# A two-layer attention block on one core: score and max matmuls on 64-row halves of the TensorE array

## The chip, the cores and the metric

One core of a Trainium2 chip runs the whole program. The metric is device time in microseconds. The kernel before took 3601.7 us (median of 3 runs, 3600.24 to 3606.74).

## What is computed

Two layers over 2048 latent tokens and 256 context tokens of width 1024. In each layer one projection feeds four branches of 256 columns: MLA attention (4 heads), GQA attention (4 heads, 2 key heads), a chunked gMLP and a Fourier mix. Each is multiplied by a gate, and one output projection follows. The change touches attention alone:

```python
def attend(q, k, v):
    ...
        s = jnp.einsum("bqkgd,blkd->bkgql", qblk, k).astype(jnp.float32) * scale
        pr = jax.nn.softmax(s, axis=-1).astype(v.dtype)
        return jnp.einsum("bkgql,blkd->bqkgd", pr, v)
```

Latent queries read latent and context keys (2304) in one softmax; in the first layer context queries read the context keys as well. An MLA head has 64 plain and 32 rotary columns in query and key, a GQA head has 64; values have 64 columns in both. The scores must be close to fp32, since the gains are large.

## The kernel before, in words

**Stages.** A layer projects its tokens (gMLP, MLA, GQA, gates, Fourier input), writes queries, keys, values and gates to DRAM (`QKA`, `QB`, `KB`, `V1`, `V2`, `G`), runs `attention()` (L1071), and then projects the output (`out_block`, L1268). Queries and keys are kept as a high and a low part, both in a format that TensorE takes in one pass ("fp32r"), so that a score is q_hi k_hi + q_lo k_hi + q_hi k_lo.

**Blocks.** Attention goes through 16 blocks per layer (L1005): four pairs of heads (pairs 0 and 1 MLA, 2 and 3 GQA) by four blocks of 512 queries. A block loops over 18 key tiles of 128 keys (L1212). For each key tile and each of the two heads e of the pair, `scores` (L1115) makes a 128x512 score in a PSUM bank of tag "s" (three banks), and ACT takes its exponential into a tile `p`. An MLA head needs three matmuls of 96 or 100 rows. A GQA head puts q_hi and q_lo on 128 rows over k_hi twice, so it needs two matmuls, of 128 and 68 rows. Four of the rows (two for a context block) hold minus the row maximum on the query's side and ones on the key's side, so the maximum is subtracted in the matmul.

**Maximum.** The maximum for block n+1 is worked out during block n: `max_units` (L952) makes one unit for each head, each of four query tiles and each of five key chunks (four of 512, one of 256): one matmul into a bank "m" (three banks) and one `reduce_max` on VectorE (L976), with a small reduce after five of them (L980). `row` (L989) transposes the maxima with TensorE and writes them negated into the query tile.

**Values and sums.** After every third key tile `drain` (L1154) runs the value matmuls of these three tiles (L1110): the two heads write partitions 0 to 63 and 64 to 127 of one bank "o" (two banks). The exponentials are added up over the key tiles in `acc` (`sums`, L1139): 34 adds per block, 6 (MLA) or 8 (GQA) on VectorE, the others on GpSimd. `fin` (L1159) sums `acc` over partitions with a matmul of ones, ACT copies that, VectorE takes the reciprocal in two halves (L1170) and multiplies by the values (L1174), GpSimd multiplies by the gate (L1175), and the result goes to DRAM.

**Order.** On TensorE, VectorE and GpSimd the order of instructions in the attention is the program's order (L1246). Max units and, in the first three blocks, units of the Fourier branch (`fnet`, L725) are spread between the score steps as `fill` (L1218). The previous block's `fin` stands after key tile 5 and its tail is spread over the steps behind. In the first layer the last block of each pair also carries a small block of the context queries (`ctx_units`). All DMAs are issued on SP's queue. `prep` (L1007) loads a pair's keys (`load_k`, L902) and a block's queries (`load_q`, L938); the first block's are loaded during the projection stage before, where its max units run as well (L1062 to L1068).

Of the kernel before, what the change touches and what calls it, by code (L numbers as in the profile page):

```python
# [28 lines left out]
PBUF = 10  # L29

# [6 lines left out]
def kernel(  # L37
# [13 lines left out]
    ps = ctx.enter_context(tc.tile_pool(name="ps", bufs=1, space=PSUM))  # L51
# [23 lines left out]
    NB = {"s": 3, "m": 3, "o": 2}  # L75

    def bank(tag, shape):
        return ps.tile(shape, F32, tag=tag, name=f"ps_{tag}", bufs=NB[tag])

# [3 lines left out]
    def f32(ap):  # L83
        return ap.bitcast(F32)
# [293 lines left out]
    def layer(l, xin, shs, hxs, xss, c):  # L378
# [511 lines left out]
        def load_kc():  # L890
            kv.a = big([100, 8, 256], F32R)
            load(f32(kv.a)[0:96], KA[:, :, SEQ:T])
            load(f32(kv.a)[96:100].rearrange("o a b -> o (a b)"), onesd)

        def load_kbc():
            kv.b = wk("kb2", [P, 2, 2, 256], F32R, bufs=1)
            load(f32(kv.b)[0:64, 0], KB[0:64, :, 0, SEQ:T])
            load(f32(kv.b)[64:128, 0], KB[0:64, :, 0, SEQ:T])
            load(f32(kv.b)[0:64, 1], KB[:, :, 1, SEQ:T])
            load(f32(kv.b)[64:68, 1].rearrange("o a b -> o (a b)"), onesd[:, 0:512])  # L900

        def load_k(pair):  # L902
            r = W()
            r.pair = pair
            if pair < 2:
                kh, kl = [], []
                for e in range(2):
                    h = 2 * pair + e
                    t = big([100, SEQ], F32R)
                    load(f32(t)[0:96], KA[:, 2 * h, 0:SEQ])  # L910
                    load(f32(t)[96:100], onesd)
                    kh.append(t)
                    t = big([96, SEQ], F32R)
                    load(f32(t), KA[0:96, 2 * h + 1, 0:SEQ])
                    kl.append(t)

                def kk(e, sel, rows, s0, n):
                    if s0 < SEQ:
                        return (kl if sel == "l" else kh)[e][0:rows, s0:s0 + n]
                    h = 2 * pair + e  # L920
                    return kv.a[0:rows, 2 * h + (sel == "l"), s0 - SEQ:s0 - SEQ + n]
            else:
                g = pair - 2
                t1 = big([P, SEQ], F32R)
                load(f32(t1)[0:64], KB[0:64, g, 0, 0:SEQ])
                load(f32(t1)[64:128], KB[0:64, g, 0, 0:SEQ])
                t2 = big([68, SEQ], F32R)
                load(f32(t2)[0:64], KB[:, g, 1, 0:SEQ])
                load(f32(t2)[64:68], onesd)

                def kk(e, sel, rows, s0, n):
                    if s0 < SEQ:
                        return (t2 if sel == "l" else t1)[0:rows, s0:s0 + n]
                    return kv.b[0:rows, int(sel == "l"), g, s0 - SEQ:s0 - SEQ + n]
            r.kk = kk
            return r

        def load_q(pair, q0, nq):  # L938
            qt = big([P, 4, 512], F32R)
            if pair < 2:  # L940
                load(f32(qt)[0:96, :, :nq], QA[:, 4 * pair:4 * pair + 4, q0:q0 + nq])
            else:
                g = pair - 2
                hs = slice(2 * g, 2 * g + 2)
                load(f32(qt)[0:64, 0::2, :nq], QB[:, hs, 0, q0:q0 + nq])
                load(f32(qt)[64:128, 0::2, :nq], QB[:, hs, 1, q0:q0 + nq])
                load(f32(qt)[0:64, 1::2, :nq], QB[:, hs, 0, q0:q0 + nq])
            return qt
# [3 lines left out]
        def max_units(blk, qt):  # L952
            kp, q0, nq, keys = blk
            pair = kp.pair
            units = []
            if len(keys) == 18:
                chunks = [(i * 512, 512) for i in range(4)] + [(SEQ, 256)]
            else:
                chunks = [(SEQ, 256)]
            nch = len(chunks)  # L960
            for e in range(2):
                mt = sm(4)

                def one(e, qi, mt):
                    mx = sm(5)
                    ops = []
                    for ci, (s0, n) in enumerate(chunks):
                        def f(ci=ci, s0=s0, n=n):
                            pm = bank("m", [P, 512])
                            rows = 96 if pair < 2 else P  # L970
                            nc.tensor.matmul(  # L971
                                pm[:, :n], qt[0:rows, 2 * e, qi * P:(qi + 1) * P],
                                kp.kk(e, "h", rows, s0, n), start=True, stop=True,
                            )
                            dst = mx[:, ci:ci + 1] if nch > 1 else mt[:, qi:qi + 1]
                            nc.vector.reduce_max(out=dst, in_=pm[:, :n], axis=AX.X)  # L976
                        ops.append(f)
                    if nch > 1:
                        def g():
                            nc.vector.reduce_max(out=mt[:, qi:qi + 1], in_=mx[:, 0:nch], axis=AX.X)  # L980
# [472 lines left out]
```

## Time and profile before

| | |
|---|---|
| median of 3 runs | 3601.7 us |
| the profiled execution | 3603.65 us |
| its span in the trace | 3601.9 us |
| TensorE busy | 94% |
| VectorE, GpSimd, ScalarE busy | 58%, 50%, 35% |
| mean granted TensorE clock | 0.974 of full |

The span runs from the first to the last instruction that the profiler shows. A TensorE instruction's end is modelled: in a dense stream the next one begins before it, and the distance from start to start is what one costs. PEld is the loading of weights on TensorE. SPq, POOLq and the like are an engine's sequencer, which issues DMAs. "L1127" is a line of the kernel before; "A" is any tile of the large arena, "s" a small one.

### The profile page before, as it was taken

The numbers are of one execution on the slowest core, as the hardware profiler recorded it, in microseconds if no ns is written. First come the engines' busy times: TensorE is split into PE (matmuls) and PEld (weight loads), VectorE is DVE, ScalarE is ACT, GpSimd is POOL, SyncE is SP. The second block draws the span as 40 slices with busy tenths as digits, with TensorE's granted clock in tenths as the row PEclk, the third lists the DMA queues.
The fourth block names the chain that finished last, engine by engine and source line by source line (L and its number), as shares of the span: only waits on it lengthen the run. The fifth ranks groups of instructions, "written<-read, shape, count | busy, mean of one in ns | idle before, by whom it ended". The sixth has DMA issues, their size and how long they took to land. (4 is left out here: it accounts for less than half of the span.)

```text
span 3601.9 us, 44855 instructions
## 1 busy us (share of the span) xinstructions
PE 3370.7 (94%) x15660; PEld 2373.4 (66%) x15660; DVE 2090.4 (58%) x3694; ACT 1278.0 (35%) x2616; POOL 1818.1 (50%) x1660
## 2 busy tenths in 40 slices
PE   6999999999999999899999998999999999999999
PEld 4888788665656555455778877876555655555487
DVE  4374337359866677784343744362887666778631
ACT  4253324113234344443123534330333444444410
POOL 2433233216566678775334334242455677877722
PEclk9999999999999999999999999999999999999999
DMA  6154314751251120003351443156314212001132
GB/s 214 37 139 128 110 45 130 240 171 59 84 123 30 29 72 24 26 12 118 139 167 46 131 129 112 50 140 177 133 50 115 62 28 73 18 21 35 40 129 92
DMA packets 252609, 331.34 MB, mean 92 GB/s; under 512 B 21408, under 2 KB 168352, under 8 KB 247720
## 3 DMA queue, kind: packets, MB, share of 16 engines
q1 hardware_dynamic: 252384, 328.49, 30.7%
q8 instruction: 123, 2.02, 0.2%
q14 instruction: 102, 0.84, 0.1%
HBM read 222.22 MB, written 106.20 MB: 91 GB/s over the span
## 5 line engine op out<-in xcount | busy, mean ns | idle before, releaser
L1151 POOL TENSOR_TENSOR acc<-acc,p 128x512 f32<-128x512 f32 x800 | 1058.9, 1343 | 407.7 <-ACT p L1132 235.0
L1132 ACT ACTIVATE p<-ps_s 128x512 f32<-128x512 f32 (+1 forms) x1168 | 681.0, 595 | 968.7 <-PE ps_s L1127 927.8
L976 DVE TENSOR_REDUCE s<-ps_m 128x1 f32<-128x512 f32 (+1 forms) x1296 | 767.0, 626 | 265.3 <-PE ps_m L971 256.4
L1127 PE MATMUL ps_s<-A 96*128 96x512 f32 (+2 forms) x2776 | 835.7, 408 | 1.6 <-ACT p L1132 0.9
L1127 PEld LDWEIGHTS ps_s<-A 96*128 96x128 f32 (+2 forms) x2776 | 498.5, 191 | 255.3 <-issue 157.5
L1110 PE MATMUL ps_o<-p,A 128*64 128x512 f32 x2048 | 494.9, 615 | 0.0
L971 PE MATMUL ps_m<-A 128*128 128x512 f32 (+2 forms) x1160 | 433.3, 401 | 61.1 <-DVE s L976 54.4
L358 PE MATMUL ps_s<-A 128*128 128x512 f32 (+1 forms) x864 | 336.9, 390 | 14.3 <-DVE sg L392 6.3
L360 PE MATMUL ps_s<-A 128*128 128x512 f32 (+1 forms) x864 | 334.0, 387 | 7.0 <-POOL A L343 7.0
L359 PE MATMUL ps_s<-A 128*128 128x512 f32 (+1 forms) x864 | 333.4, 386 | 0.0
L971 PEld LDWEIGHTS ps_m<-A 96*128 96x128 f32 (+1 forms) x1160 | 221.6, 191 | 167.3 <-DVE s L976 113.5
L1151 DVE TENSOR_TENSOR acc<-acc,p 128x512 f32<-128x512 f32 x224 | 249.1, 1112 | 120.4 <-POOL acc L1151 90.9
L1110 PEld LDWEIGHTS ps_o<-p,A 128*64 128x64 f32 x2048 | 142.0, 140 | 258.2 <-issue 256.0
L352 PE MATMUL ps_s<-A 128*128 128x256 f32 (+2 forms) x848 | 292.0, 345 | 3.5 <-ACT vst L629 1.3
L353 PE MATMUL ps_s<-A 128*128 128x256 f32 (+2 forms) x848 | 286.8, 338 | 1.9 <-POOL A L327 1.6
L354 PE MATMUL ps_s<-A 128*128 128x256 f32 (+2 forms) x848 | 284.4, 336 | 2.9 <-POOL A L308 2.9
L1304 POOL TENSOR_TENSOR A<-A,d 128x512 f32<-128x512 f32 x68 | 88.7, 1306 | 266.0 <-DVE d L1303 250.2
L308 POOL TENSOR_TENSOR A<-t,A 128x512 fp32r<-128x512 f32 (+1 forms) x80 | 100.6, 1264 | 231.1 <-DVE A L307 223.4
L1296 PE MATMUL ps_s<-A 128*128 128x512 f32 x544 | 212.5, 391 | 1.3 <-ACT A L1277 1.2
L1298 PE MATMUL ps_s<-A 128*128 128x512 f32 x544 | 211.7, 390 | 0.0
L1297 PE MATMUL ps_s<-A 128*128 128x512 f32 x544 | 211.5, 389 | 0.0
L358 PEld LDWEIGHTS ps_s<-A 128*128 128x128 f32 x864 | 167.6, 194 | 54.2 <-DVE sg L392 9.3
(188 smaller groups left out, 4562.5 us busy)
## 6 DMA issues: line engine op xcount, KB each, us to landing
st<-in_w_in SPq DMA_DIRECT2D x144, 256.0 KB, 3.0
QKA<-A SPq DMA_DIRECT2D x34, 768.0 KB, 5.5
A<-QKA SPq DMA_DIRECT2D x34, 768.0 KB, 7.0
A<-in_w_mod SPq DMA_DIRECT2D x24, 1024.0 KB, 7.9
A<-X SPq DMA_DIRECT2D x17, 1024.0 KB, 6.9
A<-in_x SPq DMA_DIRECT2D x16, 1024.0 KB, 5.1
st<-Y SPq DMA_DIRECT2D x64, 256.0 KB, 3.5
G<-sg SPq DMA_DIRECT2D x48, 256.0 KB, 2.3
```

The lines of the kernel that those rows point to most:

```text
L352: nc.tensor.matmul(pt[:, :n], hx(0, k)[:, js], hi(k), start=(k == 0), stop=False)
L353: nc.tensor.matmul(pt[:, :n], hx(0, k)[:, js], lo(k), start=False, stop=False)
L354: nc.tensor.matmul(pt[:, :n], hx(1, k)[:, js], hi(k), start=False, stop=(k == KD - 1))
L358: nc.tensor.matmul(pt[:, :n], wt[:, 0, k, :], hx(0, k), start=(k == 0), stop=False)
L359: nc.tensor.matmul(pt[:, :n], wt[:, 0, k, :], hx(1, k), start=False, stop=False)
L360: nc.tensor.matmul(pt[:, :n], wt[:, 1, k, :], hx(0, k), start=False, stop=(k == KD - 1))
L971: nc.tensor.matmul(pm[:, :n], qt[0:rows, 2 * e, qi * P:(qi + 1) * P], kp.kk(e, "h", rows, s0, n), start=True, stop=True,)
L976: nc.vector.reduce_max(out=dst, in_=pm[:, :n], axis=AX.X)
L1110: nc.tensor.matmul(z.po[64 * e:64 * e + 64, :nq], vtile(pair, e, keys[i]), pts[e][:, :nq], start=(i == 0), stop=(i == nk - 1),)
L1127: nc.tensor.matmul(s[:, :nq], kp.kk(e, sel, rows, k0, P), qt[0:rows, qi, :nq], start=(m == 0), stop=(m == len(seq) - 1),)
L1132: nc.scalar.activation(p[:, :nq], s[:, :nq], AF.Exp, bias=0.0, scale=1.0)
L1151: eng.tensor_tensor(z.acc[e][:, :nq], old[:, :nq], p[:, :nq], op=ALU.add)
```

## The change

Each pair's two heads now lie on the two halves of the partitions: head e on partitions 64e to 64e+63, for queries and keys, high and low part. Every score and max matmul has at most 64 rows, and the matmuls of the two heads are issued in turn, into one bank each.

- **Scores** (`scores(i)`, both heads at once): an MLA score has five matmuls per head: plain columns hi x hi, q_lo x k_hi, q_hi x k_lo; the rotary columns as 32 high and 32 low rows in one; and the rotary q_hi x k_lo together with the rows of the maximum (36 rows). A GQA score has four: the three products of 64 rows, and one of 36 rows with only the maximum (its keys are the constant tile `kv.z`).
- **Max units** come in pairs of heads, 18 units per block: 16 of one query tile and 512 keys for both heads (MLA four matmuls, GQA two, two banks, two reduces), and 2 of two query tiles and 256 keys. GQA maxima are of the high parts alone. The row of the maximum is made at the end of the block for both heads.
- **Banks** during the attention: four "s" (were three), three "m", one "o" (were two). ACT copies the values from PSUM into a tile `po` after a block's last drain. The PSUM pool is closed and opened anew around the attention.
- **Sums**: in the first three blocks all 34 adds are on GpSimd; later 5 (MLA) or 8 (GQA) are on VectorE, those of key tiles 2, 5, 8, 11 and 14.
- **Loads**: an MLA pair's keys take 12 DMAs (6 before), the context keys 24 (2 before), an MLA query block 8 (1 before), a GQA query block 4 (3 before). The gate is loaded in `fin`.

```diff
+        def load_mla_k(dst, pair, s0, n):
+            for e in range(2):
+                h, b0 = 2 * pair + e, 64 * e
+                d = [f32(t)[b0:b0 + 64] for t in dst]
+                s = slice(s0, s0 + n)
+                load(d[0], KA[0:64, 2 * h, s])
+                load(d[1], KA[0:64, 2 * h + 1, s])
+                load(d[2][0:32], KA[64:96, 2 * h, s])
+                load(d[2][32:64], KA[64:96, 2 * h, s])
+                load(d[3][0:32], KA[64:96, 2 * h + 1, s])
+                load(d[3][32:36], onesd[:, 0:n])
...
+            def mm(pm, c0, qi, s0, n):
+                seq = (0, 2) if pair < 2 else (0,)
+                for sel in seq:
+                    for e in range(2):
+                        nc.tensor.matmul(
+                            pm[e][:, c0:c0 + n], qt[64 * e:64 * e + 64, sel, qi * P:(qi + 1) * P],
+                            kp.kk(e, sel, 64, s0, n), start=(sel == 0), stop=(sel == seq[-1]),
+                        )
+            def chunk(qi, ci, mx):
+                pm = new()
+                mm(pm, 0, qi, ci * 512, 512)
+                for e in range(2):
+                    nc.vector.reduce_max(out=mx[:, qi % 2, e, ci:ci + 1], in_=pm[e], axis=AX.X)
...
-                        seq = (("h", 96 + nqt, 2 * e), ("h", 96, 2 * e + 1), ("l", 96, 2 * e))
+                        seq = ((0, 0, 64), (0, 1, 64), (1, 0, 64), (2, 2, 64), (3, 3, 32 + nqt))
                     else:
-                        seq = (("h", P, 2 * e), ("l", 64 + nqt, 2 * e + 1))
-                    for m, (sel, rows, qi) in enumerate(seq):
-                        nc.tensor.matmul(
-                            s[:, :nq], kp.kk(e, sel, rows, k0, P), qt[0:rows, qi, :nq],
-                            start=(m == 0), stop=(m == len(seq) - 1),
-                        )
+                        seq = ((0, 0, 64), (0, 1, 64), (1, 0, 64), (2, 2, 32 + nqt))
+                    for m, (sel, qi, rows) in enumerate(seq):
+                        for e in range(2):
+                            nc.tensor.matmul(
+                                ss[e][:, :nq], kp.kk(e, sel, rows, k0, P),
+                                qt[64 * e:64 * e + rows, qi, :nq],
+                                start=(m == 0), stop=(m == len(seq) - 1),
+                            )
...
+                    if z.pend[-1][0] == nk - 1:
+                        z.ps = wk("po", [P, 512])
+                        nc.scalar.copy(z.ps[:, :nq], z.po[:, :nq])
...
+                dve = {(i, 1) for i in (2, 5, 8, 11, 14)}
                 if n < 3:
...
+                    dve = set()
+                elif pair >= 2:
+                    dve |= {(i, 0) for i in (2, 8, 14)}
...
                 for i in range(18):
...
+                    z.scores(i)
+                    want = min(len(fill), -(-len(fill) * (i + 1) // 17))
+                    while done < want:
+                        fill[done]()
+                        done += 1
+                    z.sums(i - 1)
...
+        banks_close()
+        banks_open(f"pa{l}", s=4, m=3, o=1)
         with scope(f"a{l}"), tc.manual_schedule(engines=ordered):
             attention()
+        banks_close()
+        banks_open(f"pp{l + 1}", **PROJ)
```

## Rows read from the trace of the kernel before

**Rows 1.** The page: busy time of each engine, share of the span, instructions.

```profile
PE 3370.7 (94%) x15660; PEld 2373.4 (66%) x15660; DVE 2090.4 (58%) x3694; ACT 1278.0 (35%) x2616; POOL 1818.1 (50%) x1660
```

**Rows 2.** Windows: us, busy PE PEld DVE ACT POOL, clock, DMA (Fourier, MLA, GQA block).

```profile
877.51:944.95 67.44, 60.58 (x259) 35.67 (x259) 58.51 (x87) 22.11 (x37) 40.83 (x30) 0.97 0.16 51
...
2880.65:2933.78 53.13, 52.58 (x226) 32.12 (x227) 35.00 (x60) 22.10 (x38) 36.47 (x30) 1.00 0.12 30
3091.04:3138.43 47.39, 45.24 (x191) 25.06 (x191) 38.11 (x62) 22.66 (x39) 38.14 (x30) 1.00 0.07 23
```

**Rows 3.** Chain of waits, 2800 to 2940 us (MLA): start, us, what.

```profile
by line: PE ps_s L1127 43.4%; PE ps_o L1110 30.8%; PE ps_m L971 13.7%; DVE s L976 3.7%; DVE rd L1170 2.4%; PE ps_m L1162 2.3%; DVE acc L1151 1.9%; issue 1.7%; PE ps_m L993 0.4%
...
2809.62 2.73 PE ps_o L1110 x12
2812.34 0.90 PE ps_s L1127 x3
```

**Rows 4.** Chain of waits, 3060 to 3190 us (GQA).

```profile
by line: PE ps_o L1110 29.0%; PE ps_s L1127 23.9%; DVE s L976 14.2%; PE ps_m L971 12.5%; DVE acc L1151 6.4%; issue 4.0%; POOL acc L1151 3.2%; DVE rd L1170 2.5%; PE ps_m L1162 2.5%; DVE A L995 0.5%; DVE s L980 0.5%; ACT p L1132 0.5%; PE ps_m
...
3091.04 1.08 PE ps_m L1162 x4
```

**Rows 5.** Timeline in an MLA block: start, us, engine, line, operation, tiles.

```profile
2850.95 0.39 PE L971 MATMUL ps_m<-A 96*128 96x512 f32 x1
...
2851.18 0.86 PE L1127 MATMUL ps_s<-A 100*128 100x512 f32 x3
...
2851.88 0.39 PE L971 MATMUL ps_m<-A 96*128 96x512 f32 x1
...
2852.31 0.69 DVE L976 TENSOR_REDUCE s<-ps_m 128x1 f32<-128x512 f32 x1 [0.21 <-PE ps_m L971]
...
2852.81 0.28 PE L971 MATMUL ps_m<-A 96*128 96x256 f32 x1
...
2852.93 0.39 PE L1127 MATMUL ps_s<-A 100*128 100x512 f32 x1
```

**Rows 6.** Timeline: a drain's first weight loads, and the score behind it.

```profile
2846.26 0.20 PEld L1110 LDWEIGHTS ps_o<-p,A 128*64 128x64 f32 x4 [0.25 <-issue]
...
2848.98 0.97 PE L1127 MATMUL ps_s<-A 100*128 100x512 f32 x3
```

**Rows 7.** Weight loads by shape, whole span: busy us, mean ns.

```profile
L1127 PEld LDWEIGHTS ps_s<-A 96*128 96x128 f32 x1168 | 223.8, 192 | 41.7
...
L1127 PEld LDWEIGHTS ps_s<-A 68*128 68x128 f32 x512 | 98.0, 191 | 14.1
```

**Rows 8.** Timeline in a projection stage: 256-column matmuls.

```profile
137.38 0.28 PE L353 MATMUL ps_s<-A 128*128 128x256 f32 x1
137.50 0.28 PE L354 MATMUL ps_s<-A 128*128 128x256 f32 x1
```

**Rows 9.** Groups in the GQA block 3091.04 to 3138.43: busy us, mean ns | idle before.

```profile
L976 DVE TENSOR_REDUCE s<-ps_m 128x1 f32<-128x512 f32 (+1 forms) x41 | 23.7, 621 | 4.6 <-PE ps_m L971 4.5
...
L1166 ACT COPY rd<-ps_m 128x512 f32<-128x512 f32 x1 | 0.6, 586 | 1.3 <-PE ps_m L1162 1.3
```

**Rows 10.** Groups in the Fourier block 877.51 to 944.95.

```profile
L1151 DVE TENSOR_TENSOR acc<-acc,p 128x512 f32<-128x512 f32 x6 | 5.2, 869 | 2.6 <-POOL acc L1151 2.6
...
L1151 POOL TENSOR_TENSOR acc<-acc,p 128x512 f32<-128x512 f32 x27 | 38.3, 1435 | 27.3 <-ACT p L1132 16.6 <-DVE acc L1151 10.6
```

**Rows 11.** Waits in the same Fourier block: us, times, longest.

```profile
PEld ps_m L971 <- DVE s L976: 8.4, 11, 2.0
```

**Rows 12.** Timeline of SP's queue before the attention and at a pair switch.

```profile
711.83 0.34 SPq L892 DMA_DIRECT2D A<-QKA  x1
...
740.89 1.07 SPq L341 DMA_DIRECT2D st<-in_w_in  x2
...
988.31 0.39 SPq L910 DMA_DIRECT2D A<-QKA  x1
```

**Rows 13.** Timeline of TensorE at the switch to the second pair.

```profile
1002.11 0.50 PE L971 MATMUL ps_m<-A 96*128 96x512 f32 x1 [2.04 <-DMA A<-QKA]
```

More of the change, by code (lines that the diff above doesn't have):

```diff
@@ new lines, in max_units, with row @@
+            units = []
+            for q2 in range(0, nqt, 2):
+                mx = None
+                if len(keys) == 18:
+                    mx = sm(20).rearrange("p (a e c) -> p a e c", a=2, e=2)
+                    units += [
+                        lambda qi=qi, ci=ci, mx=mx: chunk(qi, ci, mx)
+                        for qi in (q2, q2 + 1) for ci in range(4)
+                    ]
+                units.append(lambda q2=q2, mx=mx: tail(q2, mx))
+            def row():
+                px = bank("m", [P, 512])
+                for e in range(2):
+                    nc.tensor.transpose(px[0:nqt, e * P:(e + 1) * P], mt[:, 4 * e:4 * e + nqt], ident)
+                for e in range(2):
+                    r = 64 * e + 32
+                    dst = qt[r:r + nqt, 3 if pair < 2 else 2, :nq].rearrange("r (a t) -> r a t", a=nqt)
@@ L999, in row @@
                     )
[L1000 to L1003 removed]
+            return units, row
         blocks = [(pair, qb) for pair in range(4) for qb in range(4)]
@@ L1113, in av, with scores @@
                         )
[L1115 to L1120 removed]
+                def scores(i):
+                    ss = [bank("s", [P, 512]) for _ in range(2)]
                     k0 = keys[i] * P
                     if pair < 2:
[L1123 removed]
+                        seq = ((0, 0, 64), (0, 1, 64), (1, 0, 64), (2, 2, 64), (3, 3, 32 + nqt))
@@ L1141, in sums @@
+                    pts = []
+                    for e in range(2):
+                        p = wk("p", [P, 512], bufs=PBUF)
+                        nc.scalar.activation(p[:, :nq], ss[e][:, :nq], AF.Exp, bias=0.0, scale=1.0)
+                        pts.append(p)
+                    z.pend.append((i, pts))
+                    z.sum.append((i, pts))
+                def sums(upto):
+                    while z.sum and z.sum[0][0] <= upto:
+                        i, pts = z.sum.pop(0)
                         for e, p in enumerate(pts):
@@ L1184, in ctx_units @@
                 z = main_units(blk, qt)
-                return mu + [row] + [
-                    lambda i=i, e=e: z.scores(i, e) for i in range(2) for e in range(2)
-                ] + [z.sums, z.drain], z
+                return mu + [row] + [lambda i=i: z.scores(i) for i in range(2)] + [
+                    lambda: (z.sums(1), z.drain("m"))
+                ], z
             nxt = first_max
```

216 lines of the change are left out of this document (83 added, 133 removed).

## The prediction
> **What bounds the kernel now.** I read the page first: TensorE is busy 3370.7 of 3601.9 us, no other engine over 58% [rows 1]. "Busy" is modelled here, so I then read the attention stage, the only one the change touches, block by block. Sixteen blocks per layer: eight of the MLA heads (the first three also carry the Fourier work; I call these Fourier blocks), then eight of the GQA heads. One Fourier block lasts 67.44 us, a plain MLA block 53.13, a GQA block 47.39, at a granted clock of 0.97, 1.00 and 1.00 (2.4 GHz) [rows 2]. The chain of waits over plain MLA blocks is 90% TensorE [rows 3]; over GQA blocks VectorE has some 23% of it (14.2 + 6.4 + 2.5) [rows 4].
>
> What TensorE's time consists of is read from start to start, not from durations. Four matmuls of 512 columns (three of a score, one of a max) take 2850.95 to 2851.88 = 0.93 us, so a **slot is 0.2325 us**; a 256-column one takes 2852.81 to 2852.93 = 0.12 [rows 5]. A drain of values, twelve matmuls, takes 2.72 us up to the next score [rows 3], that is 0.45 per pair: the two heads' 64-column halves run side by side already, and its first four weight loads fit into 0.20 us [rows 6]. Now the sum. An MLA block: scores 18 x 6 = 108 slots, max 32 slots and 8 halves (36), together 144 x 0.2325 = 33.5 us; six drains 16.3; sums and transposes 1.3 (the sums' 1.08 in [rows 4]). That is 51.1 of 53.13, so 2.0 us of waiting. A GQA block: 72 + 36 = 108 slots = 25.1 us, with 17.6 the same makes 42.7 of 47.39: 4.7 us of waiting. A Fourier block has 51.1 and about 3.5 of Fourier matmuls, so 12.8 us of waiting.
>
> **The change part by part.** *Scores.* An MLA score goes from three matmuls per head (six slots) to five 64-row matmuls per head, ten in five pairs. If a pair costs one slot, 18 x (6 - 5) = 18 slots per MLA block are saved. A GQA score goes from four slots to four pairs: nothing. *Max.* An MLA unit takes two pairs where two slots stood: nothing. A GQA unit takes one pair where two slots stood: (32 + 8/2) - (16 + 4/2) = 18 slots per GQA block. So 16 x 18 + 16 x 18 = 576 slots x 0.2325 = **-134 us** over both layers.
>
> All of this hangs on what a pair costs. No row shows two 64-row matmuls. Bounds: below, one slot, 0.2325 (nearest row: the column halves, which run side by side in [rows 6]); above, both in turn, 0.465. I take 0.2325, since the column halves are nearest in kind, and there even the loads overlap. What could spoil it is the loads: every pair needs two. A weight load of 96 or 68 rows takes 192 and 191 ns [rows 7], so fewer rows do not make it shorter, and 256-column matmuls, each with a load, start every 0.12 us [rows 8], so a load occupies at most 0.12. Two in turn are at most 0.24, about the slot. "TensorE: Matmul & The Clock Gate" of the Trainium skill (LDWEIGHTS) says the same against this change: the time goes by columns, not rows, P/1.2 ns. By it I estimate 107 ns a load and 213 a pair: inside the slot of a 512-column pair, but not of a 256-column one; by that page the sum would be 8 x 0.09 us worse per MLA block, half that per GQA block, some 17 us in all.
>
> The break-even is simple. Per layer the new program has 8 x (90 + 36 + 72 + 18) = 1728 pairs, the old 2016 slots; the change gains while a pair costs less than 0.2325 x 2016/1728 = **0.271 us**.
>
> *Mode changes.* Going from values to scores costs little now: twelve matmuls at 2.73 and the next score 2.72 after their start [rows 3]. Scores and max units are both 64-row, so there are no more changes per drain than before; bounds 0 and 0.1 us at each Fourier unit, under 2 us in all, nothing.
>
> *VectorE and GpSimd.* A block's max reduces go from 32 full, 8 half and 8 tiny to 36 full and 2 tiny: 23.7 us [rows 9] becomes 22.4 (at the mean 0.621) to 24.8 (at 0.69 [rows 5]), and six tiny ones fall away: between -2.3 and +1.1, I take -1. GQA adds stay eight on VectorE, MLA goes from six to five: nothing. So in a GQA block VectorE would have some 37 us and GpSimd 38 beside a TensorE of 38.5 [rows 2, 9]. That is tight. A unit now needs two of three max banks, and two reduces (1.24 us) are longer than a GQA step of five slots (1.16); the 0.24 us lost in three steps is caught up in the drain of 2.72. I therefore keep the 4.7 us of waiting as it is; bounds 2 and 9.
>
> In Fourier blocks all 34 adds go to GpSimd. VectorE loses six at 869 ns (5.2 us) and 2.6 us of waiting for GpSimd; GpSimd gets six at 1435 ns, 8.6 on 40.8, still far below the block [rows 2, 10]. TensorE waits there for VectorE's reduces (8.4 us of its loads' waits in [rows 11]), so a lighter VectorE shortens the block beyond the slots. Between 0 and 5.2 us for each of six blocks; I take 2.3: **-14 us**.
>
> *One values bank, ACT copy.* Each block gains one ACT copy of 0.59 us [rows 9]; ACT is busy 22.66 of 47.39 [rows 2], and the bank is needed three score steps later: hidden. If ACT were late, the first drain would wait; nothing suggests it. The last multiply now reads SBUF beside GpSimd, as the adds do that take 0.869 us [rows 10]: once per block, off the path.
>
> *DMAs.* A layer's first block issues 24 + 12 + 8 loads where 2 + 6 + 1 stood; SP takes 0.34 to 0.54 us for each [rows 12], so 35 x 0.45 = 16 us more on SP, ahead of the Fourier weights on the same queue. Between 711.83 and 741.96 SP issues only these nine loads and a few stores and weights, so most of it fits: between 0 and 16 us per layer, I take 4. At the switch to the second MLA pair a buffer comes free late (988.31) and TensorE already waits 2.04 us for a load at 1002.11 [rows 12, 13]. Now both heads' rows must be there and fourteen issues follow where four stood: 10 x 0.45, less what overlaps: 0 to 10, I take 4. Two layers: **+16 us**. GQA loads: four and four, where four and three stood: nothing. Opening and closing the banks: a wait of at most a drain at each of four places, in the range.
>
> **Sum:** -134 - 14 + 16 = -132 on the profiled execution's 3603.65 us (span 3601.9 and 1.75 around it) = 3471.6. It lies 2 us above the median of 3601.7, so the forecast for the median is **3470 us**. Blocks: plain MLA 53.1 to 48.9, GQA 47.4 to 43.2, Fourier 67.4 to 61.
>
> **Rivals.** *VectorE and GpSimd become the bound in the GQA blocks.* For: 37 and 38 us against 38.5, and VectorE in 23% of the chain now. Against: they have idle time there at present, because TensorE holds them up. If VectorE keeps its idle 9.3 us (47.4 - 38.1), a GQA block is 37 + 9.3 = 46.3 and saves 1.1, not 4.2: 16 x 3.1 = 50 us back, **3520 us**. Chance 0.15.
>
> *The pair costs more than 0.271 us* (slower). Place: every score and max. Mechanism: the second load is not hidden behind the matmul beside it. What an unhidden load costs is seen after a drain: the first score's three matmuls take 0.97 us there against 0.86 elsewhere, 0.11 more [rows 5, 6]. One such bite per pair gives 0.34: 2 x (1728 x 0.34 - 2016 x 0.2325) = +238, about **3840 us**. Against it: loads of column halves overlap. The same page of the Trainium skill (Part 3, Packing small matmuls) reports four row tiles at 3.07 times, not 4; by it I estimate 0.2325 x 4/3.07 = 0.303 a pair, +110 us; no row here shows it. Chance of this rival 0.14, the case below taken in.
>
> *The change doesn't do what it says:* the halves take turns, 0.465 a pair: 2 x (1728 x 0.465 - 468.7) = +670, **4270 us**. Speaks against: the column halves. Chance 0.03 of the 0.14.
>
> **Numbers.** A measurement of this kernel can tell about 0.2%, 7 us, from no change. Forecast 0.68; VectorE/GpSimd rival 0.15; pair over 0.271 0.14; a pair within a few ns of break-even, no change, 0.03. Faster 0.83, same 0.03, slower 0.14. Range: downwards GQA waiting at 2 (-43), Fourier blocks at their bound (-17) and DMAs free (-16) would make 3394 together, I take 3400; upwards the first rival's 3520 with page and DMA bounds on top, 3545. That leaves the slower cases out.
>
> **What would show it.** In the changed profile: a score's two heads' matmuls start within some 0.01 us of each other, and pairs follow every 0.23 us; ten score matmuls of an MLA step in 1.16 us. Plain MLA blocks at 49, GQA at 43, Fourier at 61; the first max after the pair switch some us later than now. Wrong if pairs stand over 0.27 apart, if VectorE's share of the chain over GQA blocks rises past a half, or if SP's queue delays the Fourier weights by more than a few us.

## The result, and the profile after

The changed kernel takes 3641.0 us at the median (3635.2 to 3643.7), the kernel before 3601.0 in the same runs: a ratio of 1.0106 with an interval of [1.0089, 1.0124], **slower by 1.1%** where 3.7% faster was forecast. The profiled execution has a span of 3638.0 us against 3601.9. First the page's busy times and the windows of three blocks of the same kinds as in [rows 1, 2] (us, busy PE PEld DVE ACT POOL, clock, DMA):

```profile
PE 3323.8 (91%) x18644; PEld 2325.6 (64%) x18644; DVE 2095.3 (58%) x3320; ACT 1246.7 (34%) x2652; POOL 1861.5 (51%) x1712
```

```profile
898.00:967.00 69.00, 56.97 (x373) 34.26 (x371) 57.70 (x70) 20.73 (x38) 49.34 (x36) 0.95 0.14 45
2864.80:2915.00 50.20, 48.89 (x342) 29.32 (x340) 37.08 (x49) 20.74 (x38) 37.37 (x31) 1.00 0.19 47
3115.40:3162.10 46.70, 41.91 (x264) 23.03 (x262) 36.16 (x52) 21.75 (x40) 36.85 (x30) 1.00 0.08 26
```

TensorE is busy 47 us less and the span is 36 us longer. The plain MLA block lost 2.9 us, the GQA block 0.7; the Fourier blocks rose in sum. The timeline of TensorE in an MLA block (start, us, line, tiles, count; compare [rows 5]) shows the pairs themselves:

```profile
2893.31 1.31 PE L1141 MATMUL ps_s<-A 64*128 64x512 f32 x10
2894.45 0.63 PE L973 MATMUL ps_m<-A 64*128 64x512 f32 x4
2894.92 1.31 PE L1141 MATMUL ps_s<-A 64*128 64x512 f32 x10
```

Ten score matmuls take 2893.31 to 2894.45, 1.14 us for five pairs or 0.228 a pair, four max matmuls 0.47. In the trace the two matmuls of a pair start 3 or 4 ns apart, and so do their weight loads. So the pairs do here what was forecast, and the loss is elsewhere. From the first value matmul of a block to that of the next, summed over both layers:

| part | forecast, us | measured, us |
|---|---|---|
| plain MLA, 10 intervals | -42 | -34.6 |
| GQA, 14 intervals | -59 | -4.4 |
| Fourier, 6 intervals | -38 | +20.8 |
| up to the first score, 2 layers | +4 in each layer (0 to +16) | +30.2 and +25.3 |

These make +37.3; the other stretches are 1.2 us shorter. In the second layer the last row counts from the last value matmul of the first layer.

**GQA.** The waits of the GQA block (us, times, longest), then of the same block kind before:

```profile
PEld ps_m L973 <- DVE s L985: 6.1, 7, 2.3
DVE acc L1165 <- POOL acc L1165: 5.2, 3, 1.8
...
PE ps_m L973 <- DVE s L985: 4.0, 4, 2.0
```

```profile
PEld ps_m L971 <- DVE s L976: 3.4, 5, 1.4
DVE acc L1151 <- POOL acc L1151: 3.0, 2, 1.6
...
PE ps_m L971 <- DVE s L976: 1.5, 2, 1.0
```

TensorE's max matmuls wait more for VectorE's reduces, and VectorE more for GpSimd's running sum. In the chain over GQA blocks, TensorE, which led it with 68% in [rows 4], has 11% left:

```profile
by line: issue 37.8%; POOL acc L1165 18.4%; DVE s L985 10.7%; DVE acc L1165 8.2%; PE ps_s L1141 5.2%; PE ps_o L1127 3.7%; DVE rd L1190 3.4%; DVE s L992 2.5%; DVE A L1302 2.5%; PE ps_m L973 2.2%; DMA st<-Y 1.7%; POOL A L1284 1.0%; DVE A L101
```

VectorE's share is about a quarter, as before; GpSimd's rose from 3 to 18%. For "issue" the profile shows no wait, so this chain says less than the one before.

**Fourier.** VectorE no longer adds there, and yet is busy 57.7 us where it was 58.5 [rows 2]. Groups of the Fourier block after (busy us, mean ns):

```profile
L746 DVE TENSOR_TENSOR A<-A 128x512 f32<-128x512 f32 x12 | 13.9, 1177 | 0.0
L805 DVE SCALAR_TENSOR_TENSOR A<-A 128x512 f32<-128x512 f32 x6 | 8.0, 1349 | 0.1
...
L839 DVE SCALAR_TENSOR_TENSOR A<-st,A 128x512 f32<-128x512 f32 x2 | 3.5, 1738 | 0.0
```

In the same block of the kernel before (865.1 to 934.6 us) these operations, as many of each, took 1146, 1134 and 1087 ns. TensorE waits 11.1 us there for reduces. From start to start its scores take 23.9 us (30.5 before) and its max matmuls 23.3 (16.1 before): what the pairs save, the waits in front of the max matmuls take back.

**The entry**, from the first max matmul to the first score, lies mostly in the projection stage before attention. Windows of it, kernel before and kernel after:

```profile
740.00:760.00 20.00, 17.57 (x78) 13.39 (x71) 7.94 (x20) 1.17 (x2) 5.08 (x4) 0.91 0.50 141
760.00:780.00 20.00, 20.00 (x90) 16.16 (x89) 12.76 (x27) 3.31 (x6) 0.00 (x0) 1.00 0.82 280
```

```profile
740.00:760.00 20.00, 12.51 (x53) 8.04 (x45) 3.65 (x10) 0.92 (x2) 2.51 (x2) 0.82 0.89 196
760.00:780.00 20.00, 20.00 (x53) 11.78 (x52) 7.25 (x13) 1.17 (x2) 2.55 (x2) 0.67 0.35 128
```

TensorE idles for keys (3.55 us, timeline below, and 1.5 us more behind it); from 756.3 to 773.3 us the granted clock is at the lower of its two levels, 1.2 of 2.4 GHz, and in the second window 53 matmuls run where 90 ran. Then the max units stand among 128-row matmuls, and both heads' rows must be complete before the first score (kernel after, SyncE's queue in the second line; then kernel before):

```profile
756.22 0.77 PE L973 MATMUL ps_m<-A 64*128 64x512 f32 x1 [3.55 <-DMA A<-QKA]
756.19 1.23 SPq L346 DMA_DIRECT2D st<-in_w_in  x2
...
778.22 0.40 PE L713 MATMUL ps_o<-A,f 128*128 128x512 f32 x1
778.54 0.73 PE L973 MATMUL ps_m<-A 64*128 64x512 f32 x2
779.20 0.50 PE L714 MATMUL ps_o<-A,f 128*128 128x512 f32 x1
779.63 0.73 PE L973 MATMUL ps_m<-A 64*128 64x512 f32 x2
...
816.28 0.38 PE L1013 MATMUL ps_m<-ident,s 128*4 128x128 f32 x2 [1.59 <-DVE s L997]
818.29 1.22 PE L1141 MATMUL ps_s<-A 64*128 64x512 f32 x4 [1.63 <-DVE A L1017]
```

```profile
787.36 0.86 PE L971 MATMUL ps_m<-A 96*128 96x512 f32 x3
788.05 0.63 PE L1127 MATMUL ps_s<-A 100*128 100x512 f32 x2
788.54 0.39 PE L971 MATMUL ps_m<-A 96*128 96x256 f32 x1
...
790.26 0.27 PE L993 MATMUL ps_m<-ident,s 128*4 128x128 f32 x1 [1.10 <-DVE s L980]
```

At 778.54 two max matmuls of one head run without partner: with one 128-row matmul they take 778.54 to 779.63, 1.09 us, and not three slots of 0.2325. The Fourier weights are issued at 756.19 us, where [rows 12] had 740.89. From first max to first score it is 62.1 us (first layer) and 58.3, where it was 36.6 and 36.7. Before, 39 of the 40 max matmuls of both heads stood ahead of the first score and took 8.75 us; only the second head's row came behind it (790.26). An MLA unit now has two max matmuls per head, so both heads have 80; only 16 and 20 of the 40 pairs start together, and the 80 take 24.1 and 21.7 us.

### The profile page after: what moved, and what is told of

It reads as the page before. It is cut to its first block, busy times and chain, and to the rows that moved or that the text cites. A ratio compares the mean times of both kernels' runs of the same rounds, so it can differ in the third digit from the quotient of the medians.

```text
span 3638.0 us, 50869 instructions
## 1 busy us (share of the span) xinstructions
PE 3323.8 (91%) x18644; PEld 2325.6 (64%) x18644; DVE 2095.3 (58%) x3320; ACT 1246.7 (34%) x2652; POOL 1861.5 (51%) x1712
## 5 line engine op out<-in xcount | busy, mean ns | idle before, releaser
L1165 POOL TENSOR_TENSOR acc<-acc,p 128x512 f32<-128x512 f32 x846 | 1101.9, 1336 | 326.1 <-ACT p L1149 302.6
L1149 ACT ACTIVATE p<-ps_s 128x512 f32<-128x512 f32 (+1 forms) x1168 | 629.4, 593 | 924.6 <-PE ps_s L1141 870.6
L985 DVE TENSOR_REDUCE s<-ps_m 128x1 f32<-128x512 f32 x1024 | 643.1, 679 | 265.9 <-PE ps_m L973 263.4
L1141 PE MATMUL ps_s<-A 64*128 64x512 f32 (+1 forms) x4456 | 679.8, 410 | 3.2 <-DVE A L1017 3.2
L1141 PEld LDWEIGHTS ps_s<-A 64*128 64x128 f32 x4456 | 441.6, 190 | 231.1 <-issue 161.0
L1127 PE MATMUL ps_o<-p,A 128*64 128x512 f32 x2048 | 503.8, 623 | 4.3 <-ACT p L1149 4.3
L973 PE MATMUL ps_m<-A 64*128 64x512 f32 (+1 forms) x1808 | 383.6, 407 | 104.9 <-DVE s L985 91.4
L363 PE MATMUL ps_s<-A 128*128 128x512 f32 (+1 forms) x864 | 340.3, 394 | 16.3 <-DVE A L347 6.5
L973 PEld LDWEIGHTS ps_m<-A 64*128 64x128 f32 x1808 | 223.1, 195 | 199.9 <-DVE s L985 143.8
L1165 DVE TENSOR_TENSOR acc<-acc,p 128x512 f32<-128x512 f32 x178 | 238.0, 1358 | 144.1 <-POOL acc L1165 144.0
L348 POOL TENSOR_TENSOR A<-st,A 128x512 fp32r<-128x512 f32 x64 | 84.8, 1336 | 220.5 <-DVE A L347 179.3
```

The costliest lines, as they stand in the source:

```text
L363: nc.tensor.matmul(pt[:, :n], wt[:, 0, k, :], hx(0, k), start=(k == 0), stop=False)
L973: nc.tensor.matmul(pm[e][:, c0:c0 + n], qt[64 * e:64 * e + 64, sel, qi * P:(qi + 1) * P], kp.kk(e, sel, 64, s0, n), start=(sel == 0), stop ...
L985: nc.vector.reduce_max(out=mx[:, qi % 2, e, ci:ci + 1], in_=pm[e], axis=AX.X)
L1127: nc.tensor.matmul(z.po[64 * e:64 * e + 64, :nq], vtile(pair, e, keys[i]), pts[e][:, :nq], start=(i == 0), stop=(i == nk - 1),)
L1141: nc.tensor.matmul(ss[e][:, :nq], kp.kk(e, sel, rows, k0, P), qt[64 * e:64 * e + rows, qi, :nq], start=(m == 0), stop=(m == len(seq) - 1),)
L1149: nc.scalar.activation(p[:, :nq], ss[e][:, :nq], AF.Exp, bias=0.0, scale=1.0)
```

## The experiments

Each is an edit of the changed kernel. Ratios are against the kernel before, in the same runs.

**Order of the entry's loads** (e1), **TensorE's order in the entry** (e2), **five adds back to VectorE** (e3).

```
 if hi_ == 1:
-    load_kc()
+    wts = [load_coltile(l, 2144 + P * i) for i in range(2)]
     first_max = prep_block(0)
+    load_kc()
```

> The changed kernel, with only the order of three loads before the attention changed: first the weights of the Fourier projection, then keys and queries of block 0, then the context keys. Theory (the many loads on SP's queue make the first max and these weights late, TensorE idles and its clock falls): the first score comes 10 to 16 us earlier in each layer, the kernel falls by 20 to 32 us to about 3610 to 3620. Rival (the entry is long because max matmuls are mixed with 128-row matmuls): under 4 us per layer, the kernel stays above 3630.

Ratio 1.0136 [1.0087, 1.0185]. The first score comes 5 us earlier in the first layer (813.4) and, counted from the first layer's last value matmul, 7.3 in the second: between theory and rival. The whole has nothing of it. In the first layer the first value matmul comes 7.5 us later than in the changed kernel (834.0 for 826.6), since TensorE now waits behind the first score, 3.8 us for keys and 6.4 for reduces. The last query load is issued at 754.5 us (755.1 in the changed kernel): one queue is as late whichever loads stand first.

```
+with tc.manual_schedule(engines={mybir.EngineType.PE}):
     stage_f(hxs, full, fill)
```

> The changed kernel, with TensorE's order in the Fourier projection of the second half fixed to the program's order, so that both heads' max matmuls stand next to each other and three units follow in a row. Theory (unpaired heads and a change of tiling at nearly every max matmul): from first max to first score 62 us becomes 44 to 50 in the first layer and 58 becomes 44 to 50 in the second, the kernel falls by 20 to 28 us. Rival (VectorE's reduces set the pace there): TensorE waits for banks instead, under 6 us per layer.

Ratio 1.0144 [1.0115, 1.0174]. Entry 58.9 and 57.6 us; the changes of tiling fell from 45 to 15 in the first layer, but the 80 max matmuls took 26.4 and 24.3 us, now waiting for reduces (5.9 us in the first layer, none in the changed kernel): the rival. The theory of order alone falls.

```
 if n < 3:
-    dve = set()
```

> The changed kernel, with five adds of each of the first three blocks put back on VectorE. Theory (34 adds on GpSimd slow VectorE's two-input operations on the shared data and hold the exponentials' tiles): the three blocks of a layer, 226 and 212 us together, fall by 5 to 10 us per layer. Rival (VectorE is the bound there, each add stands ahead of a reduce): they rise by 3 to 10 us per layer.

Ratio 1.0122 [1.0078, 1.0166]; Fourier blocks 73.1, 70.2, 85.9 and 72.5, 69.3, 75.6 (were 71.4, 69.0, 85.3 and 72.1, 67.1, 73.1), 3.4 and 4.9 us longer per layer: the low end of the rival, and not much more than these blocks vary under edits of the entry alone (e7: 2.5 in the first layer, e6: 4.1 in the second). Giving these five back to VectorE does not help.

**Most adds left out**, in GQA blocks (e4) and in Fourier blocks (e5).

```
+if pair >= 2 and nk == 18 and 3 <= i < 17:   # e5: if few and 3 <= i < 17
+    continue
```

> The changed kernel, leaving out in GQA blocks the adds of key tiles 3 to 16 (28 of 34 adds; a tiny constant is added to each sum so that the reciprocal stays finite). Theory (GpSimd's and VectorE's adds are the bound there now): GQA blocks fall from 46.7 to 48.4 us to 40 to 43. Rival (the max reduces with three banks for pairs are the bound, or TensorE is): they stay above 45.

> In the first three blocks of each layer (those with the Fourier step) the additions of the exponentials of key tiles 3 to 16 into the sums are left out, so fourteen of seventeen per head and slice, and a constant of a millionth is added to the sum where it is copied; the rest is the changed kernel. Theory (the two engines that add hold these blocks, GpSimd's share among them slowing VectorE's two-input operations): the blocks go from 71.4, 69.0, 85.3 and 72.1, 67.1, 73.1 us to 60 to 63 each (85.3 to about 75, its loads being late as well), some 40 us in all. Rival (the adds stand beside: the max units wait in VectorE's queue behind the Fourier step's own operations, whatever the adds do): each block stays within 3 us of what it was, some 10 us or less in all.

e4: ratio 0.9851 [0.9820, 0.9883]; e5: 0.9938 [0.9923, 0.9954], Fourier blocks 59.7, 59.2, 75.9 and 64.8, 58.3, 65.1, together 55 us less. Windows of a GQA block of e4 and of a Fourier block of e5, then two groups of the latter:

```profile
3064.90:3107.20 42.30, 40.97 (x264) 23.27 (x262) 29.21 (x46) 21.85 (x40) 8.66 (x8) 1.00 0.08 26
```

```profile
887.30:946.50 59.20, 54.42 (x373) 32.93 (x371) 48.47 (x70) 20.82 (x38) 10.49 (x8) 1.00 0.18 52
```

```profile
L746 DVE TENSOR_TENSOR A<-A 128x512 f32<-128x512 f32 x12 | 10.0, 852 | 0.0
L805 DVE SCALAR_TENSOR_TENSOR A<-A 128x512 f32<-128x512 f32 x6 | 6.2, 1049 | 0.1
```

Without the adds a GQA block is 42.3 us, under my 43.2, and a Fourier block 59.2, under my 61. In the Fourier blocks VectorE did none of these adds; its own operations on SBUF became shorter (1177 to 852, 1349 to 1049 ns) once GpSimd was quiet. Both theories hold, with two of e5's blocks 2 us above its range: the adds are what the pairs' gain ran into. Which part of their work holds the blocks these two runs do not say.

**Finer units in the entry** (e6), **a second queue** (e7), **a fourth max bank** (e8).

```
-left = [4 * len(blks)]
+left = [8 * len(blks)]      # and a drain amid each projection and after each j
```

> In the stage before attention the max units of the first block are put in one or two at a time at sixteen places of each half instead of about three at eight places, and TensorE takes its instructions in program order there. Theory (the time from the first max matmul to the first score, 62.1 and 58.3 us in the changed kernel and 36.6 and 36.7 before, is long because three units in a row wait for VectorE's reduces and for one another's banks): 44 to 50 us in both layers, 10 to 25 us off the whole. Rival (the time is set by the loads of keys and queries and by the stage's own work, and each change of the tiling costs its exposed load however the units are spread): 56 to 64 us, the whole within 6 us of 3641, or longer for twice the number of changes.

1.0091 [1.0069, 1.0114]. Entry 55.8 us in both layers, max matmuls 18.3 and 18.5: the rival's size. 35 and 36 of the 40 pairs start together now, and still each unit costs. TensorE's timeline of e6:

```profile
2575.91 0.40 PE L717 MATMUL ps_o<-A,f 128*128 128x512 f32 x1
2576.24 0.74 PE L975 MATMUL ps_m<-A 64*128 64x512 f32 x4
2576.91 0.51 PE L715 MATMUL ps_o<-A,f 128*128 128x512 f32 x1
2577.25 0.39 PE L716 MATMUL ps_o<-A,f 128*128 128x512 f32 x1
```

From 2575.91 to 2577.25 are four starts (128-row, two pairs, 128-row): 1.34 us, where four slots are 0.93. Each insertion costs 0.41 us for its two changes of tiling.

```
+load = nc.scalar.dma_start if first and e else nc.sync.dma_start
```

> The loads of the second head of a pair (first block's keys and queries, and the context keys) are issued from ScalarE's queue instead of SyncE's; nothing else differs. Theory (SyncE's queue, which issues twice as many loads before the first max matmul, makes it start late, 756.2 against 751.4 us, and the half clock of TensorE at 760 to 773 us follows from that wait): first max at 748 to 752 us, no stretch at half clock, first score 818.3 to 805 to 811. Rival (the queue is not what is waited for, the data's landing or the score heads' units are): first max and first score within 3 us of 756.2 and 818.3.

3627.9 us, 1.0058 [1.0043, 1.0073]; first max 749.6, first score 802.0 (16.3 us earlier); in the second layer the stretch from the last value matmul to the first score is 8.3 us shorter. Its executions went from 3616.6 to 3630.3 us, and the trace is of the first. The window again, in e7:

```profile
760.00:780.00 20.00, 20.00 (x79) 12.56 (x78) 10.71 (x18) 2.35 (x4) 0.00 (x0) 1.00 0.62 213
```

The clock is whole and 79 matmuls run instead of 53: SyncE's queue was the cause of the late keys and so of the low clock. It repeats: in all six runs with this edit the entry is 51.2 to 52.4 us in both layers, and the first score stands at 800.8 to 809.3 us. The 8.3 us of the second layer are less sure, since the projection stage in that stretch varies by as much among runs: e8, which leaves the entry as it is, has it 7.7 us shorter.

13.9 us remain of the first layer's 30.2 (17.0 of 25.3 in the second). For the first layer they add up, from start to start and to rounding: 10.1 for 80 max matmuls (18.8 us, 18 of 40 pairs together) where 39 took 8.75, 3.8 for the same 128-row matmuls between them (31.6 us for 27.8), 2.0 for the row, less 1.9 for a first max that is earlier than before.

```
-banks_open(f"pa{l}", s=4, m=3, o=1)
+banks_open(f"pa{l}", s=3, m=4, o=1)
```

> The attention stage takes four banks for max matmuls and three for scores, where the changed kernel has three and four; nothing else differs. Theory (a pair of max matmuls fills two of three banks at once, so that TensorE runs at most one and a half pairs ahead of VectorE's reduces): the waits of max matmuls on VectorE's reduces, 13.9 and 11.1 us in a Fourier block, fall by half, Fourier blocks 5 to 8 us shorter, GQA blocks 1 to 2. Rival (the reduces come late because VectorE is full, and a bank more only moves the wait; score pairs with one and a half pairs of banks wait for ScalarE's exponentials): Fourier blocks within 2 us, MLA and GQA blocks 2 to 6 us longer, the whole 20 to 80 us longer.

1.0151 [1.0099, 1.0202]. MLA blocks 52.9 (50.2), GQA 47.3, Fourier 76.2, 64.8, 88.3 and 71.2, 67.1, 72.0. For MLA blocks it is the rival: score pairs need two pairs of banks. GQA blocks are neither shorter nor longer (46.7 and 48.3 in the changed kernel). In the second Fourier block TensorE's waits for reduces fell from 11.1 to 3.6 us and the block by 4.2, but the blocks beside it rose by 4.8 and 3.0.

**VectorE's sums of its own** (e9). TensorE adds them to GpSimd's with one more matmul of ones.

```
+if (i, e) in dve:
+    o = z.own[e]
+    if o is None:
+        z.own[e] = p
+        continue
...
+    nc.vector.tensor_tensor(z.own[e][:, :nq], o[:, :nq], p[:, :nq], op=ALU.add)
```

> From the fourth block on, VectorE keeps a sum of its own, of some key tiles of the second head (six tiles in MLA blocks, nine in GQA blocks, so five and eight additions as in the changed kernel), and TensorE adds it to GpSimd's by one more matmul of ones per block; VectorE's additions then never wait for GpSimd's; GpSimd has one addition less. The buffers of exponentials go from ten to nine to make room. Theory (what holds the GQA blocks is that VectorE, waiting for GpSimd's running sum, keeps the reduces behind it waiting, and TensorE behind those): GQA blocks from 46.6 to 48.4 to 44 to 45.5 us, MLA blocks 50.2 to 49 to 50, the whole 25 to 45 us shorter. Rival (the two engines are short of time as such, GpSimd with 25 additions of 1.4 us and VectorE slowed beside it): GQA blocks within 1 us, the whole within 12 us.

3614.4 us, 1.0025 [1.0013, 1.0038], so some 27 us less than the changed kernel: GQA blocks 45.5, MLA 50.6. VectorE's groups in a GQA block:

```profile
L985 DVE TENSOR_REDUCE s<-ps_m 128x1 f32<-128x512 f32 x33 | 20.5, 676 | 8.0 <-PE ps_m L973 8.0
L1169 DVE TENSOR_TENSOR own<-own,p 128x512 f32<-128x512 f32 x7 | 8.7, 1246 | 0.1
```

The adds wait 0.1 us instead of 5.2, and VectorE's idle time is now spent on TensorE: the hand-over (with one addition of GpSimd's, which went too) was 1.2 to 2.9 us of a GQA block, a quarter to a half of what the block stands above e4's 42.3, though a matmul of ones came in.

**The row one place earlier** (e10).

```
-left = [4 * len(blks)]
+left = [4 * len(blks) - 1]
```

> In the stage before attention the last max units and the row of the maxima for the first block are put in one place earlier, ahead of the last products of the stage; nothing else differs. Theory (3.9 us from the last max matmul to the first score stand bare, since with both heads in one unit the row comes behind all of them): that gap is covered, first score 3 to 4 us earlier after the same first max in each layer, the whole 5 to 8 us shorter. Rival (the scheduler places the row by itself, or the products moved behind it take the same time bare): first score within 1.5 us, the whole within 4 us.

1.0107 [1.0083, 1.0132]: the row's two transposes fell from 2.01 to 0.14 us, the first score came 1.8 and 1.5 us earlier, half of the theory, and the first blocks took 75.5 and 76.9 us instead of 71.4 and 72.1. The whole gained nothing; why the first block grew stays open.

**Heads in turn** (e11).

```
-for m, (sel, qi, rows) in enumerate(seq):
-    for e in range(2):
+for e in range(2):
+    for m, (sel, qi, rows) in enumerate(seq):
```

> The score matmuls of a key tile run head by head, all of the first head's and then all of the second's, instead of in pairs; the instructions are the same ones. Theory (a pair takes one slot of 0.23 us because the two halves of the array run at the same time, and only where neighbours are on different halves): five or four slots more a step but one, where two heads meet, so 3.5 to 4.5 times 0.23 us over 18 steps, 14 to 19 us a block less what GQA blocks now wait: MLA blocks 65 to 70 us, GQA blocks 56 to 61, the whole 330 to 480 us longer. Rival (order within a step does not matter, matmuls of two halves are matched however they stand): the whole within 20 us.

3659.3 us in a single run, 18 over the changed kernel: the rival. MLA blocks 51.6 (50.2). TensorE's timeline, in program order ten score matmuls (five and five) and then four max:

```profile
2938.33 1.54 PE L1141 MATMUL ps_s<-A 64*128 64x512 f32 x9
2939.61 0.39 PE L973 MATMUL ps_m<-A 64*128 64x512 f32 x1
2939.71 0.39 PE L1141 MATMUL ps_s<-A 36*128 36x512 f32 x1
```

Max matmuls of the first half (2939.61) run ahead of the second head's last score matmul (2939.71). The halves keep pace by themselves, out of the program's order.

**Two ways to relieve GpSimd, and combinations.** e12 is e7, e9 and e10 together. In e13 the last two key tiles are summed by TensorE; e14 is e13 with e7; e15 is e9 and e7 with the last key tile summed by TensorE. e16 is e7 with sums of its own in GQA blocks alone, e17 the same with six of VectorE's adds instead of eight.

```
+if nk == 18 and i >= 16:      # e13, e14; e15: i >= 17
+    z.late[e].append(p)       # one matmul of ones for each, with the sum's
+    continue
```

> Three edits together: the second head's first loads on ScalarE's queue, VectorE's sums of its own, and the row one place earlier. Theory (each takes away a wait of its own, so that they add up): 13 to 24 us for the loads, 25 to 45 for the sums, 5 to 8 for the row, so 3565 to 3600 us, at or below the kernel before. Rival (they share a bound, and the sums alone bring nothing): 3610 to 3630 us.

3600.0 us, 0.9989 [0.9980, 0.9999]: e7's and e9's gains add up (e10 had none), at the weak end of the theory.

> The exponentials of the last two key tiles of each head and block are no longer added by GpSimd but summed by TensorE, by four more matmuls of ones per block; nothing else differs. Theory (GpSimd's and VectorE's additions hold both the GQA and the Fourier blocks): GpSimd loses four of 26 to 34 additions, 5.7 us of 36.9 to 49 in each block, TensorE gains 0.9; GQA blocks 46.6 to 48.4 become 44 to 46, Fourier blocks lose 1 to 4 us each, the whole 25 to 55 us shorter than 3641. Rival (in GQA blocks it is the hand-over between the engines' running sums in the middle of a block, and in Fourier blocks VectorE's own operations; the last additions are in nobody's way): every block within 1 us, 0.9 longer where TensorE is full, the whole 3635 to 3660 us.

3704.2 us, 1.0281 [1.0260, 1.0301]. MLA blocks 52.8, GQA 49 to 52, Fourier 72 to 89: against the theory, and worse than the rival. The groups of a GQA block:

```profile
L1169 POOL TENSOR_TENSOR acc<-acc,p 128x512 f32<-128x512 f32 x20 | 25.2, 1294 | 13.2 <-ACT p L1150 13.2
...
L1169 DVE TENSOR_TENSOR acc<-acc,p 128x512 f32<-128x512 f32 x8 | 8.7, 1116 | 5.2 <-POOL acc L1169 5.2
...
L1188 PE MATMUL ps_m<-p,ones 128*64 128x512 f32 x10 | 3.4, 592 | 0.0
```

The hand-over of 5.2 us is unchanged, GpSimd's saved time turned into waiting for exponentials (13.2 us; 8.6 in the changed kernel), and a matmul of ones is two passes of 0.43 us (TensorE's timeline: 2905.51, 2905.94, 2906.37), so I had priced the four, 1.7 us a block, at half. The other 0.9 us of an MLA block's 2.6 is not explained.

> The same two key tiles summed by TensorE, and the second head's first loads on ScalarE's queue. Theory (a wait of the entry and a wait of the blocks add up): 13 to 24 us for the loads, 25 to 55 for the sums, 3565 to 3600 us, below the kernel before. Rival (of the last run alone: the sums bring nothing): 3615 to 3635 us.

3681.0 us, 1.0216 [1.0194, 1.0238], outside both ranges, as e13 was, but 23 us under e13: the loads' gain stands by itself.

> VectorE's sums of its own, the last key tile summed by TensorE, and the second head's first loads on ScalarE's queue (without the row one place earlier). Theory (the hand-over and GpSimd's load both count, the row does not): 3600 us, which the three edits of before gave, less 0.5 to 1.5 us a block for two more of GpSimd's additions gone, 3560 to 3590 us. Rival (with the hand-over gone nothing is left in the additions): 3595 to 3610 us, 0.4 us a block for two more matmuls.

3605.2 us, 1.0007 [0.9996, 1.0018]; GQA blocks 46.3, MLA 51.5: the rival.

> VectorE's sums of its own in GQA blocks only (MLA blocks as in the changed kernel), and the second head's first loads on ScalarE's queue. Theory (the hand-over is a wait of the GQA blocks alone; in MLA blocks the extra matmul of ones is a loss of 0.4 us each, and the row one place earlier changes nothing): GQA blocks 45.5 us, MLA blocks 50.2, the whole 4 to 8 us under the three edits' 3600, so 3590 to 3598 us, under the kernel before by 0.1 to 0.4%. Rival (nine buffers of exponentials or the matmul cost elsewhere): 3598 to 3606 us.

3602.8 us, 0.9997 [0.9988, 1.0007]. MLA blocks 50.2, most GQA blocks 45.5, as the theory says, but the whole is not less than e12's. In the two traces the blocks together differ by 1.8 us; 6.6 us lie between the first layer's last value matmul and the second's first score, the stretch that varies anyway.

> As the run before, but VectorE does six additions in a GQA block and not eight, GpSimd two more. Theory (with the hand-over gone VectorE's reduces are what the max matmuls wait for, and each addition stands 1.25 us ahead of them, while GpSimd has 7 us idle): GQA blocks 44 to 45 us, the whole 8 to 20 us less than with eight. Rival (GpSimd, at 37 of 45.6 us, is full with two more, and the sum comes late for the matmuls of ones): GQA blocks 45.5 to 47 us, the whole the same or up to 20 us longer.

3596.8 us, 0.9985 [0.9976, 0.9993]: 1.2% under the changed kernel (each against the kernel before), and 0.15% under the kernel before, which is less than the 0.2% that the prediction called distinguishable; this is the best of seventeen edits. GQA blocks 45.3, between the theory's 45 and the rival's 45.5, and 6 us less than e16 where the theory had 8. Whether VectorE's adds or GpSimd's load (39.84 us busy in a block of 45.3) holds what is left stays open.

## Why the prediction was wrong, point by point

The forecast was -132 us and the change +40. The pairs did what the prediction staked everything on; the terms beside them failed. Against the table's forecasts the Fourier blocks miss by 59 us, the GQA blocks by 55, the entry by 47, the plain MLA blocks by 7.

- **"If a pair costs one slot"**: right where pairs stand together. 0.228 us against 0.2325, and 256-column pairs follow every 0.12 us (2580.98, 2581.10, 2581.22 in e6), so loads bound neither. By the Trainium skill ("TensorE: Matmul & The Clock Gate", LDWEIGHTS) two loads would have taken an estimated 213 ns; the measurement decides: the two loads of a pair start 3 to 4 ns apart, 184 ns each, so the halves load side by side. The slow rivals on the pair and on turns fall. The estimate of 0.303 a pair from Part 3 (Packing small matmuls) of that page of the Trainium skill does not hold here either.
- **Plain MLA blocks**: 50.2 for 48.9, the gain mis-sized by 1.3 us each; from start to start the max matmuls take 10.5 us there where they took 9.2 and the slots make 8.4, and the profile shows 0.9 of it as waits for reduces.
- **"I therefore keep the 4.7 us of waiting as it is"** failed, and with it the GQA blocks' gain: the waiting became 8.2 (46.7 less my 38.5 of TensorE's work), and e4 shows that 4.4 of them go with the adds. The max matmuls take 10.8 us of the block where their slots make 4.2; in e4 they take 6.8. The first rival's block of 46.3 came out, its total of 3520 did not. Half of the reason was in [rows 4]; what I left out is the order on VectorE: an add that waits for GpSimd's running sum holds the reduces behind it (e9: 1.2 to 2.9 us). That a pair in two of three banks adds to it is argued only: with four banks (e8) these blocks took 47.3 us, but there the scores had one less. My sign, VectorE's share of the chain past a half, did not appear: the share went to GpSimd.
- **"I take 2.3: -14 us"** for the Fourier blocks failed, in sign, and the pairs' slots were lost with it: I moved 8.6 us to GpSimd as if it were free. The rows of after and e5 show what GpSimd's adds cost VectorE's own operations, 0.3 to 0.6 us on those listed. But e3, with five adds back on VectorE, is no shorter, so the move alone is not the cause. e5 shows that the adds as a whole hold these blocks; why they do so more than before, when GpSimd did 28 of the 34, stays open. 12.3 of the 20.8 us are the third block of the first layer (85.3 for 73.0). There keys landed late: the last key load is issued 66.9 us after the block's first value matmul, 55.3 before, and TensorE stands 4.2 and 1.3 us ahead of the max matmuls at 1041.79 and 1043.87. That part was not tried alone; it is three times my 4 us for the pair switch, in one layer only.
- **"Between 0 and 16 us per layer, I take 4"** for the first loads failed, by most for its size: +30.2 and +25.3. The queue's share, e7's gain, is 16.3 us in the first layer of its trace, my upper bound of 16, and my sign for it, late Fourier weights, appeared (15.3 us). The other 13.9 was in no term. **"An MLA unit takes two pairs where two slots stood: nothing"** failed in this stage: the pairs mostly do not stand together, so 80 max matmuls cost 0.235 us each, about a slot, where 39 did before. On top come the changes of tiling and a row that now stands bare, since the first score waits for both heads.
- **"Mode changes ... under 2 us in all, nothing"** about holds in the attention stage (a block's value matmuls take 16.3 us before and after, the 32 Fourier matmuls of a block 3.96 us where they took 3.51), and fails in the stage ahead of it, which I did not look at: 0.41 us per insertion.
- **ACT copy and one bank for values**: right, no wait of TensorE on it appears in the blocks shown.
- **The range**: its upper end was added wrongly. 3520 with 17 us for the loads of pairs and the DMA bounds (two layers of 16 and 10 us, less the 16 counted) makes 3573, not 3545; 3641 lies above that too.

## What to carry to other kernels

A saving on the busiest engine is worth no more than the next limit allows; before counting it, ask of each engine that takes its instructions in the program's order what is queued behind its waits, and add up what two engines that work on SBUF side by side cost one another. A pair costs one slot only where the order puts its two matmuls together: look at every stage that issues them, not only at the one that was meant. Ask also what the first result of the new form needs: with two heads in a pair the first score waits for the rows of both. A running sum that two engines share was cheaper here as two sums, joined once.

## What the runs showed of the hardware

- Matmuls on different halves of the rows run side by side out of program order (e11: five and five in turn cost 0.08 us a step, 1.4 us over 18), and so do those on halves of the columns (e13: a value matmul starts at 2907.22, ahead of a matmul of ones at 2907.28 that stands before it in the program). Weight loads of a pair start 3 to 4 ns apart.
- Changing between 64-row and 128-row matmuls twice costs 0.41 us, in starts of 0.32 to 0.34 us in place of 0.23 (e6).
- VectorE's two-input operations on SBUF were 29 to 48% longer beside GpSimd's additions than without most of them (after and e5: 1349 and 1049, 1177 and 852, 1738 and 1175 ns), while reduces from PSUM stayed at 676 to 683 ns.
